# Projection stage of a hybrid encoder: queries and keys transposed as float32, split into two parts as they leave PSUM

## The chip, the cores and the metric

The kernel runs on one core of a Trainium2 chip. The core has a matrix engine (TensorE, PE in the profile; its weight loads are shown apart as PEld), a vector engine (VectorE, DVE), a scalar engine (ScalarE, ACT), a general engine (GpSimd, POOL) and a queue that issues transfers (SyncE, SP). Each works through its own instructions in order, and semaphores tie them together. Matrix products and transposes land in PSUM, which is used here in banks of 512 float32 columns; ACT and DVE read it from there. The metric is the device time of one execution, in microseconds; lower is better.

## The reference

A two-layer encoder over 1024 tokens of width 1024. Only layer 0 has the grouped-query attention to which the change belongs; the rest (cross-attention to 256 memory tokens, gated feed-forward with a convolution, and the pooling mixer of layer 1) is left as it is.

```python
qkv = h @ w_qkv                       # h: (1024, 1024), w_qkv: (1024, 1536)
q = rmsnorm(q, q_gain)                # 16 heads of 64
k = rmsnorm(k, k_gain)                # 4 heads of 64
q = apply_axial_rope(q, cos, sin) * (HEAD_DIM ** -0.5)
k = apply_axial_rope(k, cos, sin)
scores = jnp.einsum('bkgqd,bksd->bkgqs', q_blk, kt)
p = jax.nn.softmax(scores, axis=-1)
o = jnp.einsum('bkgqs,bksd->bkgqd', p, vt)
```

The inputs are float32. The kernel gets float32 accuracy out of a faster matrix format (fp32r): a float32 number is split into a high part, which is the number rounded to that format, and a low part, which is the number minus the high one. A product of two such numbers is three matrix products: high with high, high with low, low with high (`mm3`, lines 756 to 761).

## The kernel before

The projection stage makes queries, keys and values. It works in items, listed in `QKV` at the top of the file: ("K", t) and ("V", t) are the keys and values of the 128-token block t, of four heads each, and (half, g, t) are the queries of four heads of group g in block t. There are 8 items of keys, 8 of values and 32 of queries. Each item is one product of 24 matmuls into a PSUM bank (`plan_gemm`), 128 tokens by 256 columns. Eight items ("S", n) are not products but the first scores, of which only the row maxima are kept. The rows of x are read, transposed (line 900) and split beside the key items; the weights are read and split (lines 672 and 953) once for each group of four query items.

A query or key item then goes through `plan_head`: ACT squares the bank, DVE sums each head (line 1006), POOL makes the root (lines 732 and 734), DVE scales the bank into a tile `qn` (lines 1015 and 1017), DVE makes the two products of the rotation, `rb` (line 1024) and `qn` (line 1028), and POOL adds them (line 1032). The result is a tile of 128 tokens by 4 heads by 64, in float32.

The scores need queries and keys with the head's 64 values down the partitions, so they are transposed by TensorE, in pieces of 128 by 128. Before the change the split is made ahead of the transpose:

- A key tile is split by ACT (line 1052) and DVE (line 1056) into half of a slot `R`, each head's 64 values twice side by side, for the high and the low part. Four transposes turn the high parts into one bank, four more the low parts into another (line 1072); ACT copies the first bank out, DVE the second (line 1077).
- A query tile is split by ACT (line 672, called by `high`) and DVE (line 675, called by `low`) into a tile `qst`, in which high and low parts of a pair of heads alternate. Four transposes bring all of it into one bank (line 1104), and ACT copies it out (line 1110).

The turn of an item is not issued behind its own product but four items later (`LAG`, line 46): behind the product of item n, PE finds the turn of item n-4.

What order each engine works in is made by a planner (`Plan`) when the program is built. Each piece of work is added with a kind, which gives engine and cost (for instance "turn", 0.109 us a transpose; "add", DVE by elements; "scale", POOL), with what it reads and writes, and with the buffers that it takes and gives back. PE's order is that in which the pieces are added. The planner derives due times for the others from it, lets the pieces run on a model of the engines, and issues each engine's work in the order that comes out. Pools have a number of places in it: six PSUM banks ("B"), two `qn` tiles, three `qst` tiles, and so on. A piece that takes from a pool waits until a place is free.

Of the kernel before, what the change touches and what calls it, by code (L numbers as in the profile page):

```python
# [10 lines left out]
F32 = mybir.dt.float32  # L11
F32R = mybir.dt.float32r
AF = mybir.ActivationFunctionType
OP = mybir.AluOpType
# [31 lines left out]
LAG = 4  # L46
GROUPS = [(half, m) for half in range(2) for m in range(NH // 2)]
# [586 lines left out]
class Kernel:  # L634
# [140 lines left out]
    def attention(self):  # L775
# [43 lines left out]
        with tc.tile_pool(name="qk", bufs=1, reuse_waits="tile") as qk, self.psum("psq", 1, 6) as self.ps:  # L819
# [4 lines left out]
            plan = Plan(R, {}, {"scr": 6, "A": 1, "B": 6, "half": len(R.freed), "sq": 2, "qn": 2, "rb": 2, "qst": 3})  # L824
# [169 lines left out]
            def plan_head(it, kind, t, b):  # L994
# [16 lines left out]
                def scaled():  # L1011
                    at[qn] = buf("qn", 2)
# [18 lines left out]
                def both():  # L1031
                    nc.gpsimd.tensor_tensor(out=at[qn], in0=at[qn], in1=at.pop(rb), op=OP.add)  # L1032
# [6 lines left out]
                plan.add("scale", 2.4, both, [qn, rb], [qn], uses=[qn, rb])  # L1039
                return qn, q3  # L1040

            def plan_k(t, b):
                it = ("K", t)
                qn, q3 = plan_head(it, "K", t, b)
                half = ("kst", t)

                def view(h):
                    return R.hv(h).rearrange("p (h i c) -> p h i c", h=4, i=4)

                def high():  # L1050
                    at[half] = R.get_half()
                    nc.scalar.activation(view(at[half])[:, :, :2], q3()[:, :, None, :].to_broadcast([P, 4, 2, HD]), AF.Copy)

                def low():
                    kst = view(at[half])
                    nc.vector.tensor_tensor(out=kst[:, :, 2:], in0=q3()[:, :, None, :].to_broadcast([P, 4, 2, HD]),
                                            in1=kst[:, :, :2].bitcast(F32), op=OP.subtract)
                plan.add("copy", 650, high, [qn], [half], [("half", half)], [qn])
                plan.add("add", 620, low, [qn, half], [half], uses=[qn, half])
                plan.ended[half] = lambda: R.put_half(at.pop(half))  # L1060
                return lambda: plan_turn_k(t)

            def plan_turn_k(t):
                half = ("kst", t)
                for i in range(2):
                    b = ("kturned", t, i)

                    def turn(i=i, b=b):
                        kst = R.hv(at[half]).rearrange("p (h i c) -> p h i c", h=4, i=4)
                        p = at[b] = self.psB().rearrange("p (a b) -> p a b", a=4)  # L1070
                        for h in range(4):
                            nc.tensor.transpose(p[:, h, :], kst[:, h, 2 * i:2 * i + 2].rearrange("p a b -> p (a b)").bitcast(F32),
                                                self.ident)

                    def put(i=i, b=b):
                        o = R.v(K[i][t // 4], 4)[:, :, (t % 4) * P:(t % 4 + 1) * P]
                        (nc.vector.tensor_copy if i else nc.scalar.copy)(o, at.pop(b))
                    plan.add("turn", 4, turn, [half], [b], [("B", b)], [half])
                    plan.add("add" if i else "copy", 512, put, [b], [("KT", t, i)], uses=[b])

            def plan_q(it, b):
                half, g, t = it
                qn, q3 = plan_head(it, "Q", t, b)
                st = ("qst", it)

                def view(lo):
                    return at[st].rearrange("p (a l) (x c) -> p a l x c", l=2, x=2)[:, :, lo]

                def pairs():
                    return at[qn].rearrange("p (a x c) -> p a x c", a=2, x=2)  # L1090

                def high():
                    at[st] = qk.tile([P, 4, 2 * HD], F32R, name="qst", bufs=3)
                    self.high(view(0), pairs())

                def low():
                    self.low(view(0), view(1), pairs())
                plan.add("copy", 400, high, [qn], [st], [("qst", st)], [qn])
                plan.add("add", 370, low, [qn, st], [st], uses=[qn, st])

                def turn():
                    p = at["ps", it] = self.psB().rearrange("p (a b) -> p a b", a=4)
                    for h in range(4):
                        nc.tensor.transpose(p[:, h, :], at[st][:, h, :].bitcast(F32), self.ident)
                    at.pop(st)

                def put():
                    if (g, half) not in Q:
                        Q[g, half] = R.get()
                    nc.scalar.copy(R.v(Q[g, half], 4)[:, :, (t % 4) * P:(t % 4 + 1) * P], at.pop(("ps", it)))  # L1110

                def plan_turn():
                    bank = ("qturned", it)
                    plan.add("turn", 4, turn, [st], [bank], [("B", bank)], [st])
                    plan.add("copy", 512, put, [bank], [("QT", g, half, t)], uses=[bank], room=(("Q", g, half), 2))
# [1271 lines left out]
```

## Time and profile before

| | before |
|---|---|
| median of 3 runs | 2458.26 us (2457.17 to 2458.43) |
| the profiled execution | 2456.54 us |
| its span, from the first to the last instruction | 2454.7 us |
| granted TensorE clock, mean | 0.997 |
| busy: PE, PEld, DVE, ACT, POOL | 2428.4, 1970.4, 1914.2, 1211.7, 428.3 us |
| projection stage: first attention score on PE | 184.84 us |

A row of a group gives the line of the program, the engine and the operation, the tile written and the tiles read, their shapes, and the count; behind the first bar the busy time and the mean duration of one in ns, and behind the second the idle time of the engine just before these instructions, with what ended it. Line 672 and line 675 belong to helpers (`high` and `low`) that many parts of the program call, so the tiles tell which call it is: `qst` is a query's split, `R<-pB` a split on leaving PSUM, `R<-scr` and `T<-scr` a split of weights. A row of a timeline starts with its start and its duration in us, and in square brackets stands the idle time before it and its releaser. A row of a table of stretches gives start and end, the length, and the busy time of each engine with its instructions. Matmuls are pipelined, and their ends are modelled; what one costs is read from the distance of starts.

### The profile page before, as it was taken

Reading aid. Unit: us, or ns where it says so; the run is one execution under the profiler, and the core shown is the slowest. Engines: PE = TensorE matmul, PEld = TensorE weight load, DVE = VectorE, ACT = ScalarE, POOL = GpSimd, SP = SyncE. Lnnn points to the kernel's source line nnn. Section 1 sums busy time; section 2 is a strip of 40 time slices with the busy share of each in tenths; the row PEclk is TensorE's granted clock in tenths of the full one; section 3 lists DMA queues with packets and bytes.
Section 4 is the critical chain, followed back from the end, with each engine's and each line's share of the span. In section 5 each row is a group of like instructions: output and inputs, shape, how many; then the busy total and the mean of one; then the engine's idle time right before and its main releaser. Section 6 shows DMA issues by size and latency. Waiting matters only on the chain.

```text
span 2454.7 us, 34706 instructions
## 1 busy us (share of the span) xinstructions
PE 2428.4 (99%) x12814; PEld 1970.4 (80%) x12814; DVE 1914.2 (78%) x2718; ACT 1211.7 (49%) x1942; POOL 428.3 (17%) x457
## 2 busy tenths in 40 slices
PE   9999999999999999999999999999999999999998
PEld 9995555578898888888888888899888888888887
DVE  7888888737965599888889666987479888888875
ACT  6544555524544265545555325556346455545542
POOL 5666777610020100000000003002000000000001
PEclk9999999999999999999999999999999999999999
DMA  4300000233882233432368544497123333338852
GB/s 165 95 19 10 14 15 19 86 121 95 293 282 100 82 91 96 127 108 86 108 226 285 177 128 129 168 312 252 60 67 118 117 107 99 108 102 272 269 189 99
DMA packets 331614, 324.97 MB, mean 132 GB/s; under 512 B 32429, under 2 KB 264221, under 8 KB 331445
## 3 DMA queue, kind: packets, MB, share of 16 engines
q1 hardware_dynamic: 331445, 322.75, 41.1%
q8 instruction: 101, 1.65, 0.3%
q14 instruction: 68, 0.56, 0.1%
HBM read 235.10 MB, written 82.64 MB: 129 GB/s over the span
## 4 chain that ended last, share of the span: by engine, by line
PE 88%; DVE 4%; issue 3%; POOL 2%; DMA 1%; ACT 1%; SPq 0%; POOLq 0%; DVEq 0%; ACTq 0%
PE pB L759 21%; PE pB L761 21%; PE pB L760 21%; PE pT L1234 5%; PE pO L1272 5%; PE pA L761 3%; PE pA L759 3%; PE pA L760 3%; PE pS L791 2%; POOL rs L734 1%; PE pB L328 1%; DVE R L675 1%; PE pS L1308 1%; POOL qn L1032 1%; DVE nm L797 0%
## 5 line engine op out<-in xcount | busy, mean ns | idle before, releaser
L759 PE MATMUL pB<-R,R 128*128 128x512 f32 (+1 forms) x2732 | 1016.3, 372 | 2.5 <-ACT R L672 0.9
L761 PE MATMUL pB<-R,R 128*128 128x512 f32 (+1 forms) x2728 | 1008.3, 370 | 1.4 <-DVE R L675 1.3
L760 PE MATMUL pB<-R,R 128*128 128x512 f32 (+1 forms) x2732 | 1009.4, 369 | 0.2 <-DVE R L675 0.2
L759 PEld LDWEIGHTS pB<-R,R 128*128 128x128 f32 x2732 | 515.7, 189 | 93.1 <-ACT R L672 2.1
L761 PEld LDWEIGHTS pB<-R,R 128*128 128x128 f32 x2728 | 514.6, 189 | 89.7 <-DVE R L675 3.2
L760 PEld LDWEIGHTS pB<-R,R 128*128 128x128 f32 x2732 | 515.8, 189 | 86.5 <-DVE R L675 1.2
L672 ACT ACTIVATE R<-scr 128x512 fp32r<-128x512 f32 (+3 forms) x376 | 272.5, 753 | 227.8 <-DMA scr<-Gs 58.5
L732 POOL TENSOR_SCALAR ms<-ss 128x1 f32<-128x1 f32 (+2 forms) x97 | 31.9, 329 | 1646.2 <-ACT R L740 1281.8
L675 DVE TENSOR_TENSOR R<-X,R 128x512 fp32r<-128x512 f32 x374 | 252.6, 687 | 67.7 <-ACT R L672 67.1
L675 DVE TENSOR_TENSOR R<-scr,R 128x512 fp32r<-128x512 f32 (+2 forms) x332 | 282.6, 879 | 26.8 <-ACT R L672 26.4
L672 ACT ACTIVATE R<-X 128x512 fp32r<-128x512 f32 x374 | 231.8, 630 | 134.5 <-PE pB L760 66.1
L797 DVE TENSOR_REDUCE nm<-pS 128x1 f32<-128x512 f32 x240 | 153.5, 684 | 38.8 <-PE pS L791 38.1
L442 ACT COPY scr<-pB 128x512 f32<-128x512 f32 x156 | 91.1, 584 | 181.8 <-PE pB L761 174.6
L1240 ACT ACTIVATE pt<-pT 128x1024 f32<-128x1024 f32 x128 | 127.1, 1024 | 88.1 <-PE pT L1234 86.0
L1961 DVE TENSOR_TENSOR X<-pB,X 128x512 f32<-128x512 f32 (+1 forms) x145 | 99.3, 686 | 79.6 <-PE pB L761 78.8
L759 PE MATMUL pA<-R,R 128*128 128x512 f32 (+1 forms) x420 | 150.6, 359 | 0.0
L761 PE MATMUL pA<-R,R 128*128 128x512 f32 (+1 forms) x420 | 150.2, 358 | 0.0
L760 PE MATMUL pA<-R,R 128*128 128x512 f32 (+1 forms) x420 | 150.0, 357 | 0.0
L1272 PE MATMUL pO<-pt,V 128*64 128x512 f32 x512 | 123.7, 605 | 0.0
L444 DVE TENSOR_TENSOR scr<-pB,scr 128x512 f32<-128x512 f32 x156 | 107.0, 686 | 11.3 <-PE pB L761 11.0
L1234 PE MATMUL pT<-R,R 64*128 64x512 f32 x768 | 111.9, 393 | 0.2 <-ACT R L1110 0.2
L1806 DVE SCALAR_TENSOR_TENSOR scr<-scr,conv 128x1023 f32<-128x1023 f32 x66 | 84.6, 1282 | 20.8 <-ACT scr L1801 18.9
(188 smaller groups left out, 3065.6 us busy)
## 6 DMA issues: line engine op xcount, KB each, us to landing
X<-in_ffn_w_up SPq DMA_DIRECT2D x82, 512.0 KB
Gs<-X SPq DMA_DIRECT2D x105, 256.0 KB
scr<-in_ffn_w_down SPq DMA_DIRECT2D x45, 512.0 KB
scr<-Gs SPq DMA_DIRECT2D x35, 512.0 KB
scr<-in_xattn_w_kv SPq DMA_DIRECT2D x32, 512.0 KB
scr<-Gs SPq DMA_DIRECT2D x42, 384.0 KB
scr<-in_attn_w_qkv SPq DMA_DIRECT2D x22, 512.0 KB
Wt<-scr SPq DMA_DIRECT2D x44, 256.0 KB
```

The costliest lines, as they stand in the source:

```text
L442: self.nc.scalar.copy(out, p)
L444: self.nc.vector.tensor_tensor(out=out, in0=p, in1=out, op=OP.add)
L672: self.nc.scalar.activation(hi, src, AF.Copy)
L675: self.nc.vector.tensor_tensor(out=lo, in0=src, in1=hi.bitcast(F32), op=OP.subtract)
L759: mm(out, ah, bh, start=start, stop=False)
L760: mm(out, ah, bl, start=False, stop=False)
L761: mm(out, al, bh, start=False, stop=stop)
L797: nc.vector.tensor_reduce(NM[G][:, 2 * n + x.start:2 * n + x.stop], S, axis=AX.X, op=OP.max, negate=True)
L1234: nc.tensor.matmul(T[b][:, x * 512:(x + 1) * 512], left, right, start=(i, j) == (0, 0), stop=i == 2)
L1240: nc.scalar.activation(E[G, kt], T.pop(b), AF.Exp)
L1272: nc.tensor.matmul(O[G][x * HD:(x + 1) * HD], V32[:, kt, m // 2], E[G, kt][:, x * 512:(x + 1) * 512], start=kt == 0, stop=kt == NT - 1)
L1961: nc.vector.tensor_tensor(out=x, in0=banks[b][:, c], in1=x, op=OP.add)
```

## The change

Queries and keys are transposed as they are, in float32, and the split is made as they leave PSUM: ACT writes the high part from the bank (`high`), then DVE subtracts it from the bank (`low`). A query item has two transposes of its `qn` tile into half a bank and two evacuations of 256 columns. A key item's last addition on POOL writes each head twice side by side into a tile `kst` of 512 columns, which has four transposes into one bank and two evacuations of 512 columns. The tiles `qst` and the half slots for keys are gone, `qn` has four buffers instead of two, and `kst` has two. The first matrix products with the maxima still use the high part alone, and they wait for that alone.

```diff
+QN = 4
...
-            plan = Plan(R, {}, {"scr": 6, "A": 1, "B": 6, "half": len(R.freed), "sq": 2, "qn": 2, "rb": 2, "qst": 3})
+            plan = Plan(R, {}, {"scr": 6, "A": 1, "B": 6, "half": len(R.freed), "sq": 2, "qn": QN, "rb": 2, "kst": 2})
...
                 def both():
-                    nc.gpsimd.tensor_tensor(out=at[qn], in0=at[qn], in1=at.pop(rb), op=OP.add)
+                    x, y = at[qn], at.pop(rb)
+                    if kind == "Q":
+                        nc.gpsimd.tensor_tensor(out=x, in0=x, in1=y, op=OP.add)
+                        return
+                    k = at["kst", t] = qk.tile([P, 512], F32, name="kst", bufs=2)
+                    x, y = (z.rearrange("p (h c) -> p h c", h=4)[:, :, None, :].to_broadcast([P, 4, 2, HD]) for z in (x, y))
+                    nc.gpsimd.tensor_tensor(out=k.rearrange("p (h i c) -> p h i c", h=4, i=2), in0=x, in1=y, op=OP.add)
...
-                plan.add("scale", 2.4, both, [qn, rb], [qn], uses=[qn, rb])
-                return qn, q3
+                if kind == "Q":
+                    plan.add("scale", 2.4, both, [qn, rb], [qn], uses=[qn, rb])
+                else:
+                    plan.add("scale", 3.8, both, [qn, rb], [("kst", t)], [("kst", ("kst", t))], [qn, rb])
+                return qn
...
             def plan_k(t, b):
-                plan.add("copy", 650, high, [qn], [half], [("half", half)], [qn])
-                plan.add("add", 620, low, [qn, half], [half], uses=[qn, half])
...
-                    plan.add("turn", 4, turn, [half], [b], [("B", b)], [half])
-                    plan.add("add" if i else "copy", 512, put, [b], [("KT", t, i)], uses=[b])
+                def turn():
+                    k, p = at.pop(kst), self.psB()
+                    at[bank] = p.rearrange("p (a b) -> p a b", a=4)
+                    for h in range(4):
+                        nc.tensor.transpose(p[:, h * P:(h + 1) * P], k[:, h * P:(h + 1) * P], self.ident)
+
+                def put(lo):
+                    h, l = (R.v(K[i][t // 4], 4)[:, :, t % 4 * P:(t % 4 + 1) * P] for i in range(2))
+                    self.low(h, l, at.pop(bank)) if lo else self.high(h, at[bank])
+
+                def plan_turn():
+                    plan.add("turn", 4, turn, [kst], [bank], [("B", bank)], [kst])
+                    plan.add("copy", 512, partial(put, 0), [bank], [("KT", t, 0)], uses=[bank])
+                    plan.add("add", 512, partial(put, 1), [bank, ("KT", t, 0)], [("KT", t, 1)], uses=[bank])
...
             def plan_q(it, b):
-                plan.add("copy", 400, high, [qn], [st], [("qst", st)], [qn])
-                plan.add("add", 370, low, [qn, st], [st], uses=[qn, st])
...
-                    for h in range(4):
-                        nc.tensor.transpose(p[:, h, :], at[st][:, h, :].bitcast(F32), self.ident)
-                    at.pop(st)
+                    q, p = at.pop(qn), self.psB()[:, :256]
+                    at[bank] = p.rearrange("p (a b) -> p a b", a=2)
+                    for h in range(2):
+                        nc.tensor.transpose(p[:, h * P:(h + 1) * P], q[:, h * P:(h + 1) * P], self.ident)
...
-                    nc.scalar.copy(R.v(Q[g, half], 4)[:, :, (t % 4) * P:(t % 4 + 1) * P], at.pop(("ps", it)))
+                    h, l = (R.v(Q[g, half], 4)[:, i:4:2, t % 4 * P:(t % 4 + 1) * P] for i in range(2))
+                    self.low(h, l, at.pop(bank)) if lo else self.high(h, at[bank])
...
-                    plan.add("turn", 4, turn, [st], [bank], [("B", bank)], [st])
-                    plan.add("copy", 512, put, [bank], [("QT", g, half, t)], uses=[bank], room=(("Q", g, half), 2))
+                    plan.add("turn", 2, turn, [qn], [bank], [("B", bank)], [qn])
+                    plan.add("copy", 330, partial(put, 0), [bank], [("QT", g, half, t)], uses=[bank], room=(("Q", g, half), 2))
+                    plan.add("add", 330, partial(put, 1), [bank, ("QT", g, half, t)], [("QL", g, half, t)], uses=[bank])
```

More of the change, by code (lines that the diff above doesn't have):

```diff
@@ L1038, in plan_head @@
                 plan.add("add", 360, straight, [qn, tabkey], [qn], uses=[qn, *used])
-                plan.add("scale", 2.4, both, [qn, rb], [qn], uses=[qn, rb])
-                return qn, q3
-            def plan_k(t, b):
[L1043 to L1057, printed above, removed]
-                plan.add("copy", 650, high, [qn], [half], [("half", half)], [qn])
-                plan.add("add", 620, low, [qn, half], [half], uses=[qn, half])
-                plan.ended[half] = lambda: R.put_half(at.pop(half))
-                return lambda: plan_turn_k(t)
@@ L1063, in plan_turn_k @@
[L1063 to L1070, printed above, removed]
-                        for h in range(4):
[L1072 to L1077, printed above, removed]
-                    plan.add("turn", 4, turn, [half], [b], [("B", b)], [half])
-                    plan.add("add" if i else "copy", 512, put, [b], [("KT", t, i)], uses=[b])
+                if kind == "Q":
+                    plan.add("scale", 2.4, both, [qn, rb], [qn], uses=[qn, rb])
+                else:
+                    plan.add("scale", 3.8, both, [qn, rb], [("kst", t)], [("kst", ("kst", t))], [qn, rb])
@@ new lines, in plan_head @@
+                return qn
+            def plan_k(t, b):
+                plan_head(("K", t), "K", t, b)
+                kst, bank = ("kst", t), ("kturned", t)
+                def turn():
[10 more added lines that the diff above has]
+                    plan.add("add", 512, partial(put, 1), [bank, ("KT", t, 0)], [("KT", t, 1)], uses=[bank])
+                return plan_turn
@@ L1081, in plan_q @@
             def plan_q(it, b):
                 half, g, t = it
[L1083 to L1094, printed above, removed]
```

10 lines of the change are left out of this document (3 added, 7 removed).

## The prediction

> **What bounds the kernel now.** I read four views, from coarse to fine: the page, the table by stretches of time, the groups of instructions by line and shape, and the timeline of single engines at places where TensorE paused. The page first: its first line, and the busy time of each engine with its share of the span.
>
> ```profile
> span 2454.7 us, 34706 instructions
> PE 2428.4 (99%) x12814; PEld 1970.4 (80%) x12814; DVE 1914.2 (78%) x2718; ACT 1211.7 (49%) x1942; POOL 428.3 (17%) x457
> ```
>
> TensorE is busy for 99% of the span, so what takes work from it should show in the time, wherever nothing else takes over. The change lies in the projection stage alone, from the start to about 184.4 us. The table by stretches of time gives, after start and end, the length and then the busy time of PE, weight load, DVE, ACT and POOL:
>
> ```profile
> 20.00:66.00 46.00, 44.38 (x377) 43.76 (x375) 39.90 (x85) 28.01 (x62) 33.47 (x46) 1.00 0.33 107
> 66.00:110.00 44.00, 43.93 (x367) 42.89 (x368) 37.99 (x85) 23.97 (x48) 28.95 (x37) 1.00 0.28 88
> 110.00:170.00 60.00, 58.51 (x481) 55.92 (x480) 53.92 (x113) 29.09 (x60) 44.85 (x55) 1.00 0.12 36
> 170.00:184.40 14.40, 14.40 (x118) 13.44 (x118) 10.57 (x28) 5.27 (x13) 5.79 (x10) 1.00 0.05 2
> ```
>
> PE is the bound here too, 96 to 100% busy. But VectorE is close behind: 53.92 of 60 us between 110 and 170, which leaves it 6.1 us idle. That row decides how much of a gain on PE can be kept. ACT is at half load.
>
> What one transpose costs PE is read from the starts in its timeline (start, duration), because the durations of neighbours overlap. First a query's turn of 4, then a key's two turns, 8 in a row:
>
> ```profile
> 101.21 0.28 PE L761 MATMUL pB<-R,R 128*128 128x256 f32 x1
> 101.33 0.60 PE L1104 MATMUL pB<-ident,qst 128*128 128x128 f32 x4
> 101.69 0.36 PE L759 MATMUL pB<-R,R 128*128 128x256 f32 x1
> 101.89 0.28 PE L760 MATMUL pB<-R,R 128*128 128x256 f32 x1
> ...
> 80.19 1.03 PE L1072 MATMUL pB<-ident,R 128*128 128x128 f32 x8
> 80.98 0.37 PE L759 MATMUL pB<-R,R 128*128 128x256 f32 x1
> 81.19 0.28 PE L760 MATMUL pB<-R,R 128*128 128x256 f32 x1
> ```
>
> Product matmuls start 0.12 us apart (101.21 to 101.33). The 4 transposes take 0.36 us to the next product, and that product's successor comes 0.20 after it instead of 0.12: 0.44 us, 0.110 each. The 8 take 0.79 plus (0.21 - 0.12): 0.88 us, again 0.110 each. Without the late successor it is 0.36 / 4 = 0.090.
>
> **The change, part by part.** The groups by line and shape (count, then busy us and mean ns, then idle before them and its releaser) in the projection stage:
>
> ```profile
> L1104 PE MATMUL pB<-ident,qst 128*128 128x128 f32 x128 | 20.1, 274 | 1.5 <-DVE qst L675 1.5
> L1110 ACT CAST R<-pB 128x512 fp32r<-128x512 f32 x32 | 18.7, 584 | 0.9 <-PE pB L1104 0.7
> L675 DVE TENSOR_TENSOR qst<-qn,qst 128x256 fp32r<-128x256 f32 x32 | 14.3, 445 | 3.9 <-ACT qst L672 3.7
> L672 ACT ACTIVATE qst<-qn 128x256 fp32r<-128x256 f32 x32 | 13.3, 417 | 13.6 <-POOL qn L1032 13.4
> L900 PE MATMUL pB<-ident,scr 128*128 128x128 f32 x64 | 8.7, 275 | 1.3 <-ACT R L1110 1.3
> L1072 PE MATMUL pB<-ident,R 128*128 128x128 f32 x64 | 8.3, 272 | 0.0
> L1056 DVE TENSOR_TENSOR R<-qn,R 128x512 fp32r<-128x512 f32 x8 | 5.8, 719 | 0.7 <-ACT R L1052 0.6
> L1077 DVE CAST R<-pB 128x512 fp32r<-128x512 f32 x8 | 5.5, 684 | 0.0
> L675 DVE TENSOR_TENSOR R<-pB,R 128x512 fp32r<-128x512 f32 x8 | 5.3, 681 | 0.0
> L1052 ACT ACTIVATE R<-qn 128x512 fp32r<-128x512 f32 x8 | 5.1, 634 | 7.5 <-POOL qn L1032 7.5
> L675 DVE TENSOR_TENSOR R<-pB,R 128x256 fp32r<-128x256 f32 x4 | 1.7, 420 | 2.6 <-ACT R L672 2.6
> L672 ACT ACTIVATE R<-pB 128x256 fp32r<-128x256 f32 x4 | 1.5, 382 | 2.7 <-PE pB L761 2.7
> ```
>
> *Transposes.* Queries go from 128 to 64 (32 turns, two fewer each), keys from 64 to 32 (8 tiles, four fewer each): 96 less. The new ones read plain float32 tiles; the rows' turns (L900) do so already and cost 275 ns against 274 and 272, so the price per transpose stays. 96 x 0.110 = 10.6 us, at least 96 x 0.090 = 8.6. I take 10.6, since blocks of 4 and of 8 both give 0.110.
>
> *Queries, evacuation.* Out go a 417 ns split on ACT, a 445 ns one on DVE and a 584 ns copy on ACT; in come a high part from PSUM on ACT and a low part from PSUM on DVE, for which the value rows of the same size give 382 and 420. ACT loses 417 + 584 - 382 = 0.62 us per query, 20 us in all, which its half load hides; if ACT were the bound, all of it would count. DVE stays as it is: 25 ns less each, 0.8 us.
>
> The Trainium skill ("Perfetto Trace Analysis", section "Optimizing Scalar/DVE Operations") speaks against moving the split to PSUM: by its figures VectorE pays about 65 ns more of access on PSUM than on SBUF, ScalarE about 42 ns less. By it the 32 query lows would cost DVE 2.1 us more, an estimate from that page, and 17 of them 1.1 us in the tight stretch. The trace bears it out for ScalarE (382 against 417) and not for VectorE (420 against 445, 681 against 719), so the sum goes by the rows.
>
> *Keys.* DVE loses the split of 719 and the copy of 684 and gains a low of 681: 0.72 us each, 5.8 us over 8 keys, early in the stage. ACT loses about as much (634). POOL's last add now writes each head twice, 512 elements instead of 256:
>
> ```profile
> L1032 POOL TENSOR_TENSOR qn<-qn,rb 128x256 f32<-128x256 f32 x40 | 32.9, 821 | 28.7 <-DVE qn L1028 22.0 <-ACT sq L1002 4.6 <-DVE nmr L803 0.9
> L1335 POOL TENSOR_TENSOR scr<-scr 128x512 f32<-128x512 f32 x6 | 7.7, 1291 | 13.4 <-DMA scr<-inv 13.4
> ```
>
> Between 1291 ns, the contiguous add of 512 in a later stage, and twice 821, so 0.47 to 0.82 us more, 4 to 7 us of POOL over the keys. It is covered: the key's path loses 634 + 719 = 1.35 us between this add and the turn, and POOL has 12.5 us idle in the 46 before 66 us. Without that cover the keys would pay up to 6.6 us.
>
> *Pauses of PE.* Two kinds stand in the groups: 1.5 us for the query's low part (L1104) and 1.3 us for a PSUM bank (L900). An example of each on the timelines:
>
> ```profile
> 113.68 0.74 POOL L1032 TENSOR_TENSOR qn<-qn,rb 128x256 f32<-128x256 f32 x1 [0.99 <-DVE qn L1028]
> 115.82 0.41 DVE L675 TENSOR_TENSOR qst<-qn,qst 128x256 fp32r<-128x256 f32 x1
> 116.29 0.55 PE L1104 MATMUL pB<-ident,qst 128*128 128x128 f32 x3 [0.62 <-DVE qst L675]
> ...
> 63.48 1.61 POOL L1032 TENSOR_TENSOR qn<-qn,rb 128x256 f32<-128x256 f32 x1
> 65.12 0.42 ACT L672 ACTIVATE qst<-qn 128x256 fp32r<-128x256 f32 x1 [3.50 <-POOL qn L1032]
> 66.07 0.66 PE L900 MATMUL pB<-ident,scr 128*128 128x128 f32 x4 [1.27 <-ACT R L1110]
> ```
>
> In the first, POOL's add had ended at 114.42, and after the change the turn waits for that alone; PE came to the turn at 115.40 and would come some 0.9 us earlier (four turns, 0.22 each), just not too early. In the second, ACT stood 3.50 us before a split of a query that POOL had not finished, and the copy that frees the bank stood behind it in ACT's queue. The changed ACT waits for PE's turn, not for POOL. Both kinds should go: 2.8 us, or nothing if PE, now faster, meets the POOL add instead.
>
> *What is tight next.* The turns of queries between 110 and 170 (of line 1104 alone, PE's busy time and instructions), and the idle time of the two forms of DVE's scaling:
>
> ```profile
> 110.00:170.00 60.00, 10.90 (x68) 7.82 (x68) 1.00 0.12 36
> ...
> L1015 DVE SCALAR_TENSOR_TENSOR qn<-pB,first,rs 128x256 f32<-128x256 f32 x20 | 9.7, 483 | 8.7 <-POOL rs L734 8.2
> L1017 DVE TENSOR_TENSOR qn<-pB,rs 128x256 f32<-128x256 f32 x20 | 8.5, 424 | 5.8 <-POOL rs L734 5.1
> ```
>
> Those 68 transposes are 17 turns. After the change PE needs 60 - 17 x 0.22 - 1.5 (its pauses there) = 54.8 us for the same work, DVE 53.9 - 17 x 0.025 = 53.5 and what it can't drop of its 6.1 us idle, most of which is spent on POOL's roots. If half stays, the stretch takes 56.5: 1.7 us of the gain is lost, with ends 0 and 5.2 (all of the stretch's gain). Before 110 DVE has room: from 66 to 110 it falls below 38 of some 40 us, since the key turn at 80.19 is one of three there, each worth 0.72 us of DVE.
>
> *Buffers and the end.* A query's normalised tile is now held until its turn, four products on, hence 4 buffers instead of 2. Turn n-4 stands right behind product n in PE's order; DVE's scaling of item n comes later by the square, the sum and the root, and so finds its tile free. The product that ended before the turn at 101.33, quoted above, was scaled 4.1 us after it. And at the stage's end the first attention scores waited for the last copy out of a bank:
>
> ```profile
> 105.42 0.48 DVE L1015 SCALAR_TENSOR_TENSOR qn<-pB,first,rs 128x256 f32<-128x256 f32 x1 [0.57 <-POOL rs L734]
> ...
> 184.84 0.51 PE L1234 MATMUL pT<-R,R 64*128 64x512 f32 x2 [0.24 <-ACT R L1110]
> ```
>
> A turn's bank is now read twice in a row (382 + 420) instead of once (584): 0.2 us more at that place, and as much longer a hold elsewhere, against which keys need one bank instead of two. No DMA is added, removed or moved, and the later stages keep their instructions.
>
> **Sum.** -10.6 (transposes) - 2.8 (pauses) + 1.7 (DVE) + 0.2 (end) = -11.5. One us I give back for new pauses, as the order on each engine is planned anew (ends 0 and 5, about twice today's pauses): -10.5. The profiled execution took 2456.54 us, 1.84 more than its span; that makes 2446.0 for it, and 2447.8 for the median of the runs, which lies 1.72 above it.
>
> **Rivals.**
> (a) DVE, with POOL in its loop, sets the pace of the whole stage once PE is lighter. For it: 6.1 us idle in 60, nearly all of it waits for POOL. Then the stage shortens only by what DVE loses: 5.8 (keys) + 0.8 (lows) = 6.6 us, 2451.7. Against it: PE has waited for that loop for 2.8 us in all, so the loop has run at PE's pace, not at its own limit.
> (b) Slower: the longer hold of the query's tile closes a ring. DVE's scaling, in a queue in order, needs a tile that PE's turn frees; the turn needs POOL's add, and that needs DVE. A late add then stops DVE, with the sums and scalings of the next items behind. A pause like the 0.62 quoted, at every query, costs 32 x 0.62 = 19.8 against 10.6 saved: 2467.5. It decides from 10.6 / 32 = 0.33 us per query on. Against it: the 4.1 us between turn and scaling.
> (c) No difference: PE does its transposes in less time, and pauses on POOL's adds eat it: the keys' doubled ones with their cover gone (up to 6.6) and the whole gain of the stretch after 110 (5.2) take 11.8 of 13.4 us, 2456.7.
>
> **How the numbers follow.** The forecast as summed, 2443.5 to 2450: 0.57. Its lower end is -13.4 with no loss at all and another 1.4 of waits gone. (a), 2450 to 2453.3: 0.21. (c), 2453.4 to 2463: 0.12. (b): 0.10. The bounds of (c) are those of a difference below 0.2% (4.9 us), about what a measurement of this kernel can't tell from none. Faster is the forecast and (a), 0.78; same 0.12; slower 0.10. The range for 8 in 10 leaves out (b) and the upper part of (c) and goes half a us below the forecast's end: 2443 to 2456; the likeliest case alone, 2443.5 to 2450.
>
> **What would show it.** Query turns of 2 with 0.22 us between product streams, key turns of 4 with 0.44; the first attention score near 174 instead of 184.8 us; no PE wait for a query's low part; VectorE near 95% busy between 105 and 160. The prediction is wrong if PE's pauses in the stage are above 5 us, if VectorE waits at the scaling for a tile that a turn holds, or if the attention stage is longer than before.

## The result and the profile after

The changed kernel takes 2449.16 us (median of 8 runs, 2447.21 to 2451.97). The kernel before took 2457.43 in the same comparison (8 runs, 2455.33 to 2460.74). The ratio is 0.9964, with a 95% interval of 0.9954 to 0.9974: 8.3 us less, with 6.4 to 11.3 us inside the interval. The forecast, 2447.8 against 2458.26, is a ratio of 0.9957.

The span and the busy times on the page after:

```profile
span 2447.1 us, 34485 instructions
PE 2419.0 (99%) x12718; PEld 1961.6 (80%) x12718; DVE 1900.3 (78%) x2710; ACT 1188.4 (49%) x1902; POOL 425.5 (17%) x457
```

The table by stretches of time after, with the columns that it had before (start and end, length, busy time of PE, weight load, DVE, ACT and POOL, granted clock, share and rate of the transfers):

```profile
20.00:66.00 46.00, 43.64 (x360) 43.40 (x360) 34.10 (x76) 25.10 (x56) 35.70 (x49) 0.96 0.36 120
66.00:110.00 44.00, 42.85 (x354) 41.38 (x353) 38.75 (x92) 17.29 (x34) 31.94 (x41) 1.00 0.38 113
110.00:170.00 60.00, 60.00 (x493) 57.54 (x492) 52.16 (x125) 20.18 (x46) 42.99 (x59) 1.00 0.08 24
```

PE has 96 instructions fewer. From 110 to 170 it is never idle (60.00 of 60, where it was 58.51). The first stretch is new in one number: its granted clock is 0.96, where it was 1.00.

The change is best measured by the projection stage itself, from the first product on PE to the first attention score. Before, these started at 8.78 and 184.84 us, 176.06 apart; after, at 9.94 and 175.85, 165.91 apart: 10.15 us less. The profiled span fell by 7.6 (2454.7 to 2447.1), because the first product came 1.16 later and what follows the first score took 1.39 longer. Over the profiles of the experiments below, whose work outside the stage is the same, the first product starts between 8.8 and 9.7 us, so that 9.94 is the latest of all, and the part behind the first score varies by 4 us (2268.8 to 2272.9), so these two are read as scatter; no run tested that.

The turns, from PE's timeline after (a query's, a key's, then the last query's and the first attention score at L1210):

```profile
100.38 0.29 PE L762 MATMUL pB<-R,R 128*128 128x256 f32 x1
100.50 0.38 PE L1080 MATMUL pB<-ident,qn 128*128 128x128 f32 x2
100.64 0.36 PE L760 MATMUL pB<-R,R 128*128 128x256 f32 x1
100.84 0.28 PE L761 MATMUL pB<-R,R 128*128 128x256 f32 x1
...
81.14 0.60 PE L1060 MATMUL pB<-ident,kst 128*128 128x128 f32 x4
81.49 0.36 PE L760 MATMUL pB<-R,R 128*128 128x256 f32 x1
81.70 0.28 PE L761 MATMUL pB<-R,R 128*128 128x256 f32 x1
...
175.21 0.38 PE L1080 MATMUL pB<-ident,qn 128*128 128x128 f32 x2
175.52 0.50 PE L792 MATMUL pS<-R,R 64*128 64x512 f32 x2
175.85 0.86 PE L1210 MATMUL pT<-R,R 64*128 64x512 f32 x6
```

A query's turn costs 0.14 to the next product and 0.08 for its late successor, 0.22 us; a key's costs 0.35 and 0.09, 0.44 us. That is 0.110 per transpose, as before.

Since the order of the turns is the same in both kernels, their starts can be set side by side. This shows where the time went (worked out from both timelines, us):

```
turn             before   after   after - before
key 0             27.73   30.87    +3.14
key 1             35.69   39.37    +3.68
key 7             90.44   90.51    +0.07
query 11         112.09  110.40    -1.69
query 12         115.40  113.43    -1.97
query 13         119.48  116.45    -3.03
query 20         144.41  139.15    -5.26
query 21         147.66  142.18    -5.48
query 31         183.56  175.21    -8.35
first score      184.84  175.85    -8.99
```

From turn to turn the difference grows by 0.22 where nothing else happens (query 20 to 21). Over the pause that the prediction quoted at 116.29 it grows by 1.06 (query 12 to 13): the transposes' 0.22 and 0.84 for a turn that is no longer cut in two. But the changed kernel enters this part late: at the first key it stands 3.14 us behind, of which 1.16 is the start, and at the second 3.68. It takes until key 7 to be level. The cause is a pause of PE ahead of the first key's turn. The timeline after, of PE, then of POOL, of DVE and of SP's queue:

```profile
27.48 1.03 PE L901 MATMUL pB<-ident,scr 128*128 128x128 f32 x8
30.87 0.90 PE L1060 MATMUL pB<-ident,kst 128*128 128x128 f32 x3 [2.36 <-POOL kst L1039]
...
23.41 1.72 POOL L869 TENSOR_TENSOR scr<-tab,gk 128x128 f32<-128x128 f32 x4
28.50 3.55 POOL L1039 TENSOR_TENSOR kst<-qn,rb 128x512 f32<-128x512 f32 x2
...
28.41 1.28 DVE L895 SCALAR_TENSOR_TENSOR scr<-scr,rs 128x1024 f32<-128x1024 f32 x1
...
4.44 7.54 SPq L889 DMA_DIRECT2D scr<-in_x  x4
12.02 0.44 SPq L851 DMA_DIRECT2D tab<-in_rope  x1
```

And the stretch behind the pause, in the table by stretches after:

```profile
30.90:34.20 3.30, 3.30 (x16) 3.30 (x17) 1.88 (x6) 1.63 (x3) 3.02 (x5) 0.52 0.19 67
```

The same places on the timeline before, SP's queue and POOL's first work with the keys' tables:

```profile
4.19 2.36 SPq L888 DMA_DIRECT2D scr<-in_x  x2
6.59 0.56 SPq L850 DMA_DIRECT2D tab<-in_rope  x1
...
15.56 1.30 POOL L861 TENSOR_TENSOR scr<-tab,gk 128x512 f32<-128x512 f32 x1
18.71 0.89 POOL L868 TENSOR_TENSOR scr<-tab,gk 128x128 f32<-128x128 f32 x2
23.61 0.73 POOL L1032 TENSOR_TENSOR qn<-qn,rb 128x256 f32<-128x256 f32 x1 [0.89 <-DVE qn L1028]
```

The load of the rotary tables went out at 12.02 instead of 6.59, behind two more loads of rows. The planner's due time for it follows from the key's path, which lost two steps, and moved from 5.98 to 6.95 in the planner's own model; the loads of the third row block are due at 6.39. So the keys' tables, and with them the first key's addition, came 4.9 us later (23.61 to 28.50). There the addition also met a product of DVE that reads two tiles of SBUF (28.41) and took 2.32 us instead of the 1.29 that it takes with the tables first, so about 1.0 us of the pause comes from this meeting; the last experiment below is about it. PE then paid twice: the pause, and the row of 30.90 to 34.20, where the clock granted is 0.52 and 16 matmuls run in 3.30 us, which is 3.30 x 0.48 = 1.6 us more.

What the clock goes by can be read from the same trace, in stretches of 3.41 us that begin or end where the clock changed (it rose at 6.77, fell at 30.66 and rose at 34.07):

```profile
6.77:10.18 3.41, 1.79 (x15) 1.50 (x13) 1.39 (x5) 2.20 (x5) 0.00 (x0) 1.00 1.07 353
27.25:30.66 3.41, 1.26 (x12) 1.02 (x10) 3.38 (x10) 2.55 (x9) 3.24 (x4) 1.00 0.27 69
30.66:34.07 3.41, 3.20 (x15) 3.20 (x16) 2.12 (x7) 1.63 (x3) 3.13 (x6) 0.50 0.26 90
```

The clock is at half from 30.66 to 34.07, for 3.41 us, and within each of the 13 profiles the changes of the clock lie a whole number of such stretches (3.413 us) apart. Transposes count as work: PE begins with nothing but transposes, which start 0.21 us apart up to about 6.7 us and 0.11 apart from 6.85 on, so they alone brought the clock up. Of the rows above, the first two hold some 0.2 us of products each and otherwise transposes; the one with 1.62 us of idle time left the clock alone, the one with 2.15 was followed by half the clock. In the first 480 us of the 13 profiles, half the clock followed all nine such stretches in which PE was idle for 1.8 us or more and none in which it was idle for 1.5 or less; of four between 1.5 and 1.7 it followed one. Idle time is not all that counts: near 1520 us the clock also fell behind a stretch of small matrix products in which PE was busy for 2.85 of 3.40 us (kernel before).

The Trainium skill ("TensorE: Matmul & The Clock Gate", section "Part 1: The HAM clock gate") says that the clock halves after an idle window of some 3.4 us. The halving (0.50) and the 3.41 us agree. The window does not have to be idle throughout here: PE was busy for 1.26 us of it.

### The profile page after: what moved, and what is told of

It reads as the page before. It is cut to its first block, busy times and chain, and to the rows that moved or that the text cites. A ratio compares the mean times of both kernels' runs of the same rounds, so it can differ in the third digit from the quotient of the medians.

```text
span 2447.1 us, 34485 instructions
## 1 busy us (share of the span) xinstructions
PE 2419.0 (99%) x12718; PEld 1961.6 (80%) x12718; DVE 1900.3 (78%) x2710; ACT 1188.4 (49%) x1902; POOL 425.5 (17%) x457
## 4 chain that ended last, share of the span: by engine, by line
PE 90%; DVE 3%; issue 3%; DMA 2%; POOL 1%; ACT 1%; SPq 0%; POOLq 0%; DVEq 0%; ACTq 0%
PE pB L760 22%; PE pB L762 22%; PE pB L761 22%; PE pO L1248 5%; PE pT L1210 5%; PE pA L762 3%; PE pA L760 3%; PE pA L761 3%; PE pS L792 2%; PE pB L329 1%; DVE R L676 1%; PE pS L1284 1%; POOL rs L735 0%; PE pA L2249 0%; DMA scr<-X 0%
## 5 line engine op out<-in xcount | busy, mean ns | idle before, releaser
L1210 PE MATMUL pT<-R,R 64*128 64x512 f32 x768 | 112.2, 393 | 0.0
L673 ACT ACTIVATE R<-pB 128x512 fp32r<-128x512 f32 (+1 forms) x147 | 70.7, 499 | 68.3 <-PE pB L762 53.8
```

Of the source, the lines that this page charges most:

```text
L673: self.nc.scalar.activation(hi, src, AF.Copy)
L1210: nc.tensor.matmul(T[b][:, x * 512:(x + 1) * 512], left, right, start=(i, j) == (0, 0), stop=i == 2)
```

## The experiments

The stage given below is always the distance from the first product to the first attention score in the profiled execution: 176.06 before, 165.91 after. Ratios are to the kernel before, run on the same chip in the same comparison, with the 95% interval.

**Is the late table load the cause of the first pause?** One edit: the load gets a due time that puts it ahead of the third row block again.

```diff
-                    plan.add("load", 1.1, load, (), ["tab", "gQ", "gK"])
+                    plan.add("load", 1.1, load, (), ["tab", "gQ", "gK"], late=5.0)
```

> The changed kernel, with the one load of the rotary tables given back its old place ahead of the third row block in the queue of loads (a due time of 5 us). Theory 1 (the shorter path of a key made the planner let that load fall back, so POOL has the first key's tile late, PE pauses 2.4 us before the first key turn and then runs some 12 matmuls at half clock, 1.5 us): no pause, clock 1.00 between 20 and 66 us, some 4 us less than the changed kernel, about 2445. Rival (that pause is a late transfer of the one profiled execution, or comes from POOL's doubled additions): pause and time stay, 2449.

Measured: 2448.73 us (5 runs), ratio 0.9953 (0.9941 to 0.9966), stage 164.31. The load and the first key's turn on its timeline:

```profile
7.21 0.45 SPq L851 DMA_DIRECT2D tab<-in_rope  x1
...
27.12 1.03 PE L901 MATMUL pB<-ident,scr 128*128 128x128 f32 x8
27.99 0.60 PE L1060 MATMUL pB<-ident,kst 128*128 128x128 f32 x4
28.34 0.37 PE L760 MATMUL pB<-R,R 128*128 128x256 f32 x1
```

The stretch that had run at half clock, in its table by stretches:

```profile
30.90:34.20 3.30, 3.30 (x30) 3.30 (x29) 1.87 (x6) 3.03 (x5) 3.06 (x5) 1.00 0.15 48
```

The pause is gone, the clock is 1.00, and 30 matmuls run where 16 did. So the load's place is the cause of both. Some 4 us were spent there, and all of them had been expected back, yet the stage is only 1.6 us shorter: pauses of 0.56 near 42 us, 0.88 and 0.66 between 62 and 65 and 0.62 at the end, all for DVE, stand in for it, where the changed kernel has 0.42 and 0.66. A PE that arrives earlier meets DVE earlier.

The same kernel was run twice more as the partner of another one.

> The tables-first kernel again, beside the next three. Theory 2 (the first key's pause was worth 4 us on PE, but two thirds of it came back as waits for DVE at 42 and 62 us, so 1.6 us are left in the stage): 0.4 to 0.5% under the kernel before, within 2 us of the changed kernel. Rival (theory 1, all of the pause shows, and the first measurement was off): 0.5 to 0.6% under.

> The tables-first kernel a third time, in more rounds and beside the next one, as its partner. Both theories: 2447.7 to 2448.7 us, first product to first attention score 164 to 164.5 us, pauses of about 0.56 us near 42, 0.88 and 0.66 near 62 to 64 and 0.6 at the end.

Measured: 2447.68 us, ratio 0.9959 (0.9946 to 0.9971), stage 164.08; and 2446.34 us, ratio 0.9951 (0.9938 to 0.9963), stage 164.35. The stage repeats within 0.3 us. The ratios lie between 0.9951 and 0.9959, and each interval overlaps that of the changed kernel (0.9954 to 0.9974), so in the whole time this edit of 1.6 us is not told from none.

**How much comes from queries and how much from keys?** The queries as in the changed kernel, the keys as before:

```diff
-                kst, bank = ("kst", t), ("kturned", t)
+                plan.add("copy", 650, high, [qn], [half], [("half", half)], [qn])
+                plan.add("add", 620, low, [qn, half], [half], uses=[qn, half])
...
-                plan.add("turn", 4, turn, [kst], [bank], [("B", bank)], [kst])
+                plan.add("turn", 4, turn, [half], [b], [("B", b)], [half])
```

> Only the queries are changed; keys are split ahead of their transposes, as before, with eight transposes. Theory 1 (PE's transposes at 0.110 us each, and its pauses): 64 transposes less, 7.0 us, and the pauses for a query's low part, 1.5 us; the keys' path is the old one, so the load of the tables keeps its place and there is no pause at the first key: 8 to 10 us under the kernel before, about 2448. Rival (DVE sets the pace): DVE loses only 0.8 us, about 2456.5.

Measured: 2452.64 us (6 runs), ratio 0.9969 (0.9957 to 0.9981), stage 166.96. By medians that is 6.0 us under the kernel before (2458.67), less than the 8 to 10 expected, which the interval (4.7 to 10.6 us) does not exclude. In the stage the queries alone bring 9.1 us: 32 x 0.22 = 7.0 of transposes, and 2.1 that are left for pauses. The keys add 1.05 as the change has them, and 2.65 with the table load in its place (166.96 to 164.31), of the 8 x 0.44 = 3.5 that their transposes cost.

**Is it the number of transposes?** Every transpose of a query or key issued twice, into the same place of the bank, with all else of the change kept:

```diff
-                    for h in range(2):
+                    for h in (*range(2), *range(2)):
...
-                    for h in range(4):
+                    for h in (*range(4), *range(4)):
```

> The changed kernel with every transpose of queries and keys made twice in a row, the second over the first: as many transposes as before the change, all else as after it, and the planner told so. Theory 1 (the gain is PE's transposes): 96 x 0.110 = 10.6 us more than the changed kernel, about 2459.5. Rival (the gain comes from the lighter ACT and from DVE, or from the order): within 3 us of the changed kernel, 2449 to 2452.

Measured: 2457.53 us (11 runs), ratio 0.9994 (0.9985 to 1.0003), stage 175.56. With the old number of transposes the gain is gone: 9.65 us of the stage, by medians 8.4. The 10.56 put back are not all seen, because with more work on PE the pauses of 0.42 and 0.66 near 66 us disappear, and one of 0.50 at the end comes. Against the kernel before, with as many transposes, the split behind them is worth 0.5 us of stage, but this is a balance: by the starts on PE's timeline some 2.1 us of waits for low parts, 1.5 for the bank at 66 us and 0.9 for two small waits go, and the first key's turn costs 4.2 (a pause of 2.42 and half the clock). No run has the doubled transposes with the tables first.

**How much room does the loop of DVE and POOL have?** The low part of every query written twice by DVE:

```diff
+                    if lo:
+                        self.low(h, l, at[bank])
                     self.low(h, l, at.pop(bank)) if lo else self.high(h, at[bank])
```

> The changed kernel with the low part of each query computed twice by DVE, 32 instructions of 0.42 us more (spaced some 0.35), 11 us of DVE in all, and the planner told so. Theory 1 (PE is the bound and DVE has room after the change): 0 to 3 us more than the changed kernel, 2449 to 2452. Rival (DVE, with POOL in its loop, sets the pace): all of it shows, about 2460.

Measured: 2458.04 us (11 runs), ratio 0.9993 (0.9985 to 1.0002), stage 175.32. One of the new pauses, on PE's timeline:

```profile
118.55 0.44 PE L1080 MATMUL pB<-ident,qn 128*128 128x128 f32 x2 [0.62 <-POOL qn L1035]
```

The stretch from 110 to 170 in its table:

```profile
110.00:170.00 60.00, 55.88 (x440) 51.68 (x440) 54.65 (x130) 19.34 (x42) 41.07 (x55) 1.00 0.12 36
```

32 x 0.42 = 13.4 us more work on DVE make the stage 9.4 longer, though PE waited for nothing in that stretch of the changed kernel, and DVE was at 52.16 of 60. The loop stalls PE at 54.65 of 60 already: PE waits for POOL's additions, which wait for DVE. So the room left is about 4 us in the whole stage (13.4 less 9.4, an estimate).

**Does the ring of query tiles close?** Three tiles for the normalised queries, then two:

```diff
-QN = 4
+QN = 3
```

> The changed kernel with three normalised tiles instead of four. The scaling of item n then waits for the turn of item n-3, which stands behind product n+1, some 3.1 us behind the end of product n; the scaling came about that late anyway. Theory 1 (a ring with room in it): 0 to 3 us more than the changed kernel. Rival (the ring of tiles, scaling, add and turn is already tight with four): 10 us more and up, PE waiting for POOL's add at most turns.

> The changed kernel with two tiles, as many as before the change. The scaling of item n waits for the turn of item n-2, behind product n+2, 6.2 us after product n; from the scaling to the end of the add it takes about 3 to 5 us, and the turn comes 12.4 us after product n. Theory 1: the add comes just in time, but the product's PSUM bank is held 3 us longer and DVE stands before the scaling with the next items behind it: 5 to 20 us more than the changed kernel, slower than before or equal. Rival (tiles don't matter, as the planner reorders around them): within 2 us of the changed kernel.

Measured: three tiles 2448.67 us (5 runs), ratio 0.9962 (0.9950 to 0.9975), stage 166.45; two tiles 2454.5 us (11 runs), ratio 0.9990 (0.9981 to 0.9999), stage 173.77. With two, DVE's waits between 106 and 160 (what waited for what, us in total, how often, the longest):

```profile
DVE qn L1018 <- PE pB L1080: 5.1, 12, 0.8
DVE qn L1016 <- PE pB L1080: 1.6, 3, 0.7
DVE qn L1016 <- POOL rs L735: 0.9, 1, 0.9
```

One period of it on the timeline, PE and then DVE:

```profile
121.43 0.38 PE L1080 MATMUL pB<-ident,qn 128*128 128x128 f32 x2
122.49 0.36 PE L760 MATMUL pB<-T,R 128*128 128x256 f32 x1 [0.68 <-DVE qn L1018]
...
121.92 0.42 DVE L1018 TENSOR_TENSOR qn<-pB,rs 128x256 f32<-128x256 f32 x1 [0.30 <-PE pB L1080]
```

That is the ring of rival (b), in the form that the expectation gave it: DVE stands at the scaling until PE's turn has freed a tile (0.30), and PE, right behind that turn, stands for a bank that the late scaling holds (0.68). The prediction had PE wait for POOL's addition, at every query; here it waits for a bank, about once in four queries. It costs 7.3 us of stage against three tiles, 5.8 by medians on the same chip. At three tiles DVE waits for PE's turns too (4.7 and 1.2 us at its two forms of scaling between 106 and 160), but PE has no pause there; the fourth tile changes nothing that is resolved.

**Does the doubled addition on POOL cost anything?** The tables first, and POOL writes each key head once; ACT, at half load, copies it beside itself:

```diff
-                    x, y = (z.rearrange("p (h c) -> p h c", h=4)[:, :, None, :].to_broadcast([P, 4, 2, HD]) for z in (x, y))
-                    nc.gpsimd.tensor_tensor(out=k.rearrange("p (h i c) -> p h i c", h=4, i=2), in0=x, in1=y, op=OP.add)
+                    x, y = (z.rearrange("p (h c) -> p h c", h=4) for z in (x, y))
+                    nc.gpsimd.tensor_tensor(out=k.rearrange("p (h i c) -> p h i c", h=4, i=2)[:, :, 0], in0=x, in1=y, op=OP.add)
...
+                    nc.scalar.copy(k[:, :, 1], k[:, :, 0])
```

> Tables first, and POOL writes each head of a key once (256 elements), while ACT, which has room, copies it beside itself. POOL loses some 0.85 us per key (1.65 to 0.8), 6.8 in all, ACT gains some 0.4 us. Theory 2 (the pauses that are left early in the stage come from DVE's load, not from POOL's doubled add): within 1 us of tables first. Rival (the doubled add on POOL holds up the keys and through the shared roots the queries): the waits for DVE at 42 and 62 us go too, 2 to 3 us less, about 2446.

> The head written once by POOL and copied beside itself by ACT, a second time, in more rounds. Theory that the doubled add costs time though PE never waits for it by name: again 2 to 3 us below its partner, as the medians of the first pair had it (2444.99 against 2447.68). Rival, that only the stage counts: there the two traces differ by 0.85 us (163.23 against 164.08), so 0.5 to 1.2 us below its partner and the rest of the first difference was scatter between later stages.

Measured beside its partner: 2444.99 against 2447.68 us, ratios 0.9951 (0.9939 to 0.9964) against 0.9959, stage 163.23 against 164.08; and again, 2445.67 against 2446.34, ratios 0.9947 (0.9934 to 0.9959) against 0.9951, stage 164.07 against 164.35. In the stage it is the shortest version, 0.3 to 0.9 us below its partner, and its medians are the lowest of all. Its intervals overlap those of its partner and of the changed kernel (0.9954 to 0.9974), so in the whole time the order of these versions is not settled; the first pair's 2.7 us did not come again, and the second's 0.7 lies in the 0.5 to 1.2 expected from the stage alone.

**Why did DVE's work shrink between 106 and 160?** The prediction had DVE's durations unchanged. The groups there (DVE's rotation products and POOL's additions), first in the kernel before:

```profile
L1024 DVE TENSOR_TENSOR rb<-qn,tab 128x128 f32<-128x128 f32 x32 | 11.9, 411 | 0.0
L1032 POOL TENSOR_TENSOR qn<-qn,rb 128x256 f32<-128x256 f32 x16 | 11.9, 742 | 11.0 <-DVE qn L1028 8.4 <-ACT sq L1002 2.5
```

The same groups after:

```profile
L1025 DVE TENSOR_TENSOR rb<-qn,tab 128x128 f32<-128x128 f32 x32 | 7.8, 284 | 0.0
L1035 POOL TENSOR_TENSOR qn<-qn,rb 128x256 f32<-128x256 f32 x17 | 14.0, 826 | 0.0
```

The same 32 products take 4.1 us less; POOL's additions take 84 ns more each, and DVE's whole work falls from 48.17 to 45.60 us. Before, pairs of them ran beside a POOL addition (0.99 us for the pair at 113.78, beside the addition of 113.68 that the prediction quotes, against 0.48 to 0.49 in the changed kernel); in the changed order their mean is 284 ns, so hardly any is held up. To see whether that is the cause, POOL got a second addition behind each query's, on a tile that nobody reads (with three query tiles, to be compared with that run):

```diff
                         nc.gpsimd.tensor_tensor(out=x, in0=x, in1=y, op=OP.add)
+                        spare, one = qk.tile([P, 256], F32, name="spare", bufs=1), self.ident[:, None, :].to_broadcast([P, 2, P])
+                        nc.gpsimd.tensor_tensor(out=spare.rearrange("p (a b) -> p a b", a=2), in0=one, in1=one, op=OP.add)
```

> Three tiles, and behind each query's add POOL makes a second add of the same shape on a tile that nobody reads, 32 in all, so that more of VectorE's work runs beside a POOL add. Theory that VectorE and POOL slow each other on plain float32 tensor operations: between 106 and 160 the rb products rise from a mean of 282 ns to 350 ns or more, or POOL's adds rise well above 827 ns, and VectorE's busy time rises from 45.3 by 2 us or more. Rival, that the 411 ns of the kernel before came from something else (their order among other work): rb stays within 20 ns of 282, POOL's adds within 60 ns of 827. On time: POOL was busy for 38.7 of these 54 us and gets 12 to 13 more, so it is nearly full; theory that the VectorE and POOL loop is close to its limit: 2452 to 2459 us with PE waiting for POOL's adds; rival with room left: 2447 to 2450.

Measured: 2453.02 us (10 runs), ratio 0.9976 (0.9967 to 0.9985), stage 171.53 against 166.45. The duration of one in ns, as least, median and greatest, for four lines of DVE between 106 and 160:

```profile
L1025 DVE TENSOR_TENSOR rb<-qn,tab x32: 273/282/733, 109.9 to 159.6; 128x128 f32<-128x128 f32 x32
L1029 DVE TENSOR_TENSOR qn<-qn,tab x16: 406/604/866, 106.2 to 158.3; 128x256 f32<-128x256 f32 x16
L1007 DVE TENSOR_REDUCE ss<-sq x16: 404/409/415, 105.8 to 158.0; 128x4 f32<-128x256 f32 x16
L676 DVE TENSOR_TENSOR R<-pB,R x16: 409/411/422, 109.2 to 159.1; 128x256 fp32r<-128x256 f32 x16
```

Two rotation products on DVE's timeline (x2, together 0.88 us) and POOL's work beside them:

```profile
109.89 0.88 DVE L1025 TENSOR_TENSOR rb<-qn,tab 128x128 f32<-128x128 f32 x2
109.80 0.61 POOL L1037 TENSOR_TENSOR spare<-ident 128x256 f32<-128x256 f32 x1
```

The two lines of DVE that read two tiles of SBUF are stretched, up to 733 and 866 ns; the reduction (one input) and the low part (one input from PSUM) stay within 20 ns. DVE's busy time rises from 45.31 to 47.27 us, though its instructions are the same and the stretch holds fewer of them, and PE has four pauses there, of 0.47 to 0.61 us, all for POOL's additions. So the two engines hold each other up where both read tiles of SBUF, and the order decides how often. The rise of rb alone (282 to 338 ns) is less than the expectation's 350; the other product (414 to 626) took more of it. The Trainium skill ("SBUF — State Buffer", section "Who interferes with whom") states it as a rule: a DVE instruction with two SBUF inputs contends with a POOL instruction that reads SBUF, and whichever is second stands until the first is done. All four lines agree.

## Why the prediction was right, and where it was not

The side and the size were right: 2447.8 forecast, 2449.16 measured, within the range. The stage became 10.15 us shorter where 10.5 had been forecast. The single terms agree less well than their sum, which came out in part by luck:

| term of the sum | forecast | shown |
|---|---|---|
| 96 transposes | -10.6 | -10.6 (32 x 0.22 + 8 x 0.44) |
| pauses for a query's low part | -1.5 | -2.1 |
| pause for a bank at 66 us | -1.3 | 0 |
| DVE in the stretch 110 to 170 | +1.7 | 0 |
| end of the stage | +0.2 | -0.4 |
| new pauses | +1.0 | +4.0 at the first key, -0.9 for two small ones that went (at 24.18 and 31.91 before) |

The terms on the right are read from the starts on PE's timeline. They sum to -10.0; what is left lies in steps of 0.3 us and less. The first key cost 3 us more than was given back for new pauses, and the bank's 1.3 did not come; the stretch after 110, the two small pauses, the low parts and the end were better than forecast by nearly as much (1.7, 0.9, 0.6 and 0.6).

- **Transposes**: right in price and in weight. Doubling them took the gain back.
- **Low part**: right, and a little more: a turn cut in two also lost its second start (three steps of 1.06, 0.87 and 0.87 in the starts of the turns, less 0.22 each, are 2.1).
- **Bank at 66 us**: the step "both kinds should go" failed here. That the changed ACT waits for PE's turn and not for POOL holds, but DVE is next in line for the same banks (PE's timeline after):

```profile
67.37 0.41 PE L1080 MATMUL pB<-ident,qn 128*128 128x128 f32 x2 [0.42 <-DVE R L676]
68.44 0.36 PE L760 MATMUL pB<-R,R 128*128 128x256 f32 x1 [0.66 <-DVE qn L1016]
```

- **DVE after 110**: mis-sized. The sum kept its durations and let half of its idle time bind. In fact its work between 106 and 160 fell by 2.6 us, with six instructions more, as the rotation products took 4.1 less, hardly held up by POOL's additions any more; and PE had no pause above 0.1 us from 71 us to the end of the stage. That a little more would have bound is shown by the doubled low part: rival (a) was about 4 us of DVE's work away.
- **New pauses**: the one us given back stood for this kind, and the place was one that the prediction had called covered. "It is covered" holds for the amount (the first key's path did get shorter, and with the tables first its turn has no wait), but not for the order: a shorter path moved the due time of a load that feeds it, behind another load. The step that failed took the 1.35 us that the key's path loses as slack that covers the longer addition; it left out what the planner does with the saved time, and "No DMA is added, removed or moved" was wrong.
- **Keys' addition**: its price had been put between 1291 and 1642 ns. Both ends are found after the change. Five of the eight took 1262 to 1297 ns; the three that began within 0.22 us behind a row product of DVE like the one at 28.41 took 2208 to 2317, and the mean is 1654 (least, median, greatest of that line):

```profile
L1039 POOL TENSOR_TENSOR kst<-qn,rb x8: 1262/1294/2317, 28.5 to 86.3; 128x512 f32<-128x512 f32 x8
```

  Its cover is not complete: writing the head once instead gives 0.3 to 0.9 us of stage.
- **Rival (b)**: not in this kernel, where DVE waits at the scaling for POOL's roots alone. Its ring is real, though: four tiles keep it away and three would; two close it, at 7.3 us of stage and not the 19.8 of its price.
- **Of what would show it**: turns of 0.22 and 0.44 came, as did the end of waits for a low part and a first score near 174 (175.85, and 173.3 to 173.6 with the tables first). DVE near 95% between 105 and 160 did not come: 45.60 of 54 us from 106 on, 84%. PE's pauses come to 4.3 us from the first product to the first score, as in the kernel before (4.3), and to 5.9 with the wait ahead of the first product (5.6 before). The sign of 5 us did not say from where to count, so it decides nothing; but pauses that were to shrink from 2.8 us to 1.0 did not shrink, and there the step on pauses failed.

## What to carry to other kernels

Count what a change takes from the engine that is busy all the time, and price it by the distance of starts: that term held to 0.1 us. Then look at the order, not only at the durations: where a planner sets due times by path lengths, a shorter path can send the load that feeds it later, and the first item of a stage has nothing to hide that. And where DVE and POOL share a stage, note which of their instructions read two tiles of SBUF, and read the least and the median duration beside the mean.

## What had not been expected of the hardware

- A pause costs PE its own length, or up to 1.6 us more, by where it falls. The pause of 2.36 us lay within one of the stretches of 3.41 us by which the clock goes (rows above), and half the clock followed. In the run with the doubled low part, a pause of 1.93 at the first key did the same, and one of 1.68 for DVE, from 168.32 to 170.00, did not (clock 1.00 from 165 to 173): a border at 168.53 cut it, and the stretch behind that held 1.48 us of idle time.
- One DVE product of 128x128 from two SBUF tiles takes 273 ns at the least and up to 733 beside a POOL addition. The split that the change moved shows the same: reading two SBUF tiles, it took 409 to 1264 ns in the kernel before (row below). Reading PSUM, beside even more POOL work, it stayed between 409 and 422 (the fourth line of the run with the spare addition).

```profile
L675 DVE TENSOR_TENSOR qst<-qn,qst x30: 409/420/1264, 70.9 to 180.4; 128x256 fp32r<-128x256 f32 x30
```
